# Causal attention heads in a fused trunk: the division by the softmax sums on ScalarE, the second pair's transposes in later steps

## Chip, cores, metric

One Trainium2 chip, one core. The metric is the device time of one execution in microseconds; the kernel before takes 824.06 us (median of 3 runs, 823.75 to 824.91).

## What is computed

Two layers over 256 tokens of width 2048, in float32. Layer 0 mixes by trailing-window pooling, layer 1 by causal attention with 12 heads of 128 (the sequence is one block long, so the block selection of the reference picks nothing, and each query attends to the tokens up to itself). Both layers have a memory branch of 4 heads over 256 memory tokens. Cut to what matters here:

```
s = q @ k.T * HEAD_DIM**-0.5        # layer 1: masked to k_pos <= q_pos
p = softmax(s)
o = p @ v
mixed = concat([branch * silu(gate_b), mem_o * silu(gate_m)])
h = layer_norm(ALPHA * h + mixed @ w_out)
```

The causal heads need q, k, v and a gate from four projections of h; k and v have one shared weight for all B layers.

## The kernel before, in words

**Split products.** A float32 product is made of three matmuls in the type fp32r. Every operand is split by `split` (L69): ScalarE copies it to fp32r (the high part, L71), VectorE subtracts the high part from the original (the low part, L72). A product is then high x high, high x low and low x high. So each weight block passes DMA, ScalarE, VectorE and TensorE.

**Items and steps.** All weights come in items of 128x1024 (512 KB) in one list, in the order in which TensorE uses them. The main loop of `run` (L130) does one step for each item i: it splits item i+3 (LP = 3), issues the load of item i+4 on the SyncE queue (LD = 4, four `raw` buffers), issues item i's matmuls, with the epilogue of a projection if the item is its last, and then calls whatever was registered for this step by `later(n, fn)` (L92), in the order of registration. Each engine takes its instructions in this order. Nothing else orders the work.

**Causal heads.** Layer 1 does the 12 causal heads in three groups of four (the loop that calls `plan` at L686 and L687). A group has eight items for k (`w_sk`), eight for q (`w_in`), eight for the gate (`w_in`), eight for v (`w_sv`, split into the tile `xm`). Step 0 in this text is the last item of q: there `go` registers two pairs of heads, `MobaPair`, through `plan(pr, a, b, c)` (L395). Steps 1 to 8 are then the gate, steps 9 to 16 the values, and from step 17 on come the next group's keys, or after the last group the output projection. A pair has these parts:

- `a` (L353), TensorE, VectorE: scores in PSUM, the mask added (L366), row maxima (L266) and their scaling (L267).
- `exps` (L269), ScalarE: four exponentials with a per-partition bias and a running sum, from p into the tile `ebuf`.
- `divide` (L274), VectorE: one reciprocal of the sums (L275), four multiplications of `ebuf` in place (L277).
- `turn` (L346), VectorE: four transposes of 32x192 for each of four groups of partitions, from `ebuf` to p (L350).
- `b` (L373), ScalarE and VectorE: the split of the transposed probabilities of one head into ph and pl.
- `c` (L380), TensorE: the value products of both heads into o. For each head and each half m of the keys it does value-high x ph, value-high x pl, value-low x ph, so that the third and the sixth matmul are the first to read the low value parts. Then `gated` (L279) multiplies with the gate (L282) and splits into zT.

The first pair has a = 1, b = 6, c = 17, the second a = 7, b = 18, c = 20. The tiles p, ebuf, ph and pl have one buffer each.

**Memory heads.** `MemPair` (L285) has the same parts, but transposes its divided probabilities on TensorE, in `b` (L305). It runs once in each layer (`mem_q_gate`, L515), with `divide` and `gated` shared with the causal heads.

The epilogue of the gate (L232) folds two accumulators (L220 on ScalarE, L221 on VectorE) and in the next step does a tanh (L241) and a product (L242). The epilogue of the values (L247) splits each of two accumulators into the tile vv.

Of the kernel before, what the change touches and what calls it, by code (L numbers as in the profile page):

```python
# [11 lines left out]
F32 = mybir.dt.float32  # L12
F32R = mybir.dt.float32r
AF = mybir.ActivationFunctionType
ALU = mybir.AluOpType
AX = mybir.AxisListType

P = 128
T = 256
# [26 lines left out]
def trunk(ctx: ExitStack, tc: tile.TileContext, a: dict, out: bass.AP):  # L46
    nc = tc.nc
    ctx.enter_context(tc.manual_schedule())
    sb = ctx.enter_context(tc.tile_pool(name="sb", bufs=1))
# [9 lines left out]
    zT = sb.tile([P, KT, 2 * T], F32R, name="zT")  # L59
# [6 lines left out]
    def mm(o, l, r, start, stop):  # L66
        nc.tensor.matmul(o, l, r, start=start, stop=stop)  # L67

    def split(hi, lo, src):  # L69

        nc.scalar.activation(hi, src, AF.Copy)  # L71
        nc.vector.tensor_sub(lo, src, f(hi))  # L72
# [19 lines left out]
    def later(n, fn):  # L92
        events[now[0] + n].append(fn)
# [73 lines left out]
    def proj_t(mov, wblk, done):  # L167


        acc = []  # L170

        def consume(kb):
            def go(wh, wl, k0=0, k1=4):
                if not acc:
                    acc.extend(ps.tile([P, 512], F32, name="acc", bufs=4) for _ in range(2))
                h = wh.rearrange("p (k n) -> p k n", n=256)
                l = wl.rearrange("p (k n) -> p k n", n=256)
                for n in range(2):
                    s = slice(n * P, (n + 1) * P)
                    for kk in range(k0, k1):  # L180
                        k = 4 * kb + kk
                        if k < KT - 1:
                            mm(acc[n], h[:, kk, s], mov[:, k], k == 0, False)
                        mm(acc[n][:, :T], l[:, kk, s], mov[:, k, :T], False, False)
                        if k == KT - 1:
                            mm(acc[n], h[:, kk, s], mov[:, k], False, True)
                    if kb == 3:
                        done(n, acc[n])
            return go
        for kb in range(4):  # L190
            item(wblk[kb], BLK, consume(kb))
# [31 lines left out]
    def to_heads(dst, base):  # L223
        def done(n, acc):
            s = sb.tile([P, T], F32, name="fold", bufs=3)
            hi, lo = dst()[:, base + n, :T], dst()[:, base + n, T:]
            fold(s, acc)
            nc.vector.tensor_copy(hi, s)
            nc.vector.tensor_sub(lo, s, f(hi))
        return done  # L230

    def to_gate(dst, base):  # L232

        def done(n, acc):
            s = sb.tile([P, T], F32, name="fold", bufs=3)
            fold(s, acc)
            g = dst()

            def finish():
                th = sb.tile([P, T], F32, name="th", bufs=2)  # L240
                nc.scalar.activation(th, s, AF.Tanh, scale=0.5)  # L241
                nc.vector.scalar_tensor_tensor(g[:, base + n, :], th, 1.0, s,  # L242
                                               op0=ALU.add, op1=ALU.mult)
            later(1, finish)
        return done

    def to_values(dst):  # L247
        def done(t, acc):
            split(dst()[:, t, 0], dst()[:, t, 1], acc)
        return done  # L250

    def heads_tile(name):
        return sb.tile([P, 4, 2 * T], F32R, name=name)


    class Rows:
# [17 lines left out]
        def divide(self):  # L274
            nc.vector.reciprocal(self.sm, self.sm)  # L275
            for c, (src, dst) in enumerate(self.rows):
                nc.vector.tensor_scalar_mul(dst, dst, self.sm[:, c:c + 1])  # L277

    def gated(o, g, kt):  # L279

        zf = sb.tile([P, T], F32, name="zf", bufs=3)
        nc.vector.scalar_tensor_tensor(zf, o, 0.5, g, op0=ALU.mult, op1=ALU.mult)  # L282
        split(zT[:, kt, :T], zT[:, kt, T:], zf)

    class MemPair(Rows):  # L285
        def __init__(self, h0, st):
# [29 lines left out]
        def c(self):  # L316
            v, g = self.st["v"], self.st["g"]
            o = ps.tile([P, 2, T], F32, name="o")
            for j in range(2):
                h = self.h0 + j  # L320
                for m in range(2):
                    vh = v[:, m, 0, h * HD:(h + 1) * HD]
                    vl = v[:, m, 1, h * HD:(h + 1) * HD]
                    s = slice(m * T, (m + 1) * T)
                    mm(o[:, j], vh, self.ph[:, j, s], m == 0, False)
                    mm(o[:, j], vh, self.pl[:, j, s], False, False)
                    mm(o[:, j], vl, self.ph[:, j, s], False, m == 1)
            for j in range(2):
                gated(o[:, j], g[:, self.h0 + j, :], 12 + self.h0 + j)

    class MobaPair(Rows):

# [47 lines left out]
        def c(self):  # L380
            v, g = self.st["v"], self.st["g"]
            o = ps.tile([P, 2, T], F32, name="o")
            for j in range(2):
                h = self.h0 + j

                for m, (d, s) in enumerate(((o[:, j], slice(0, T)), (o[:, j, P:], slice(T, 384)))):
                    vh = v[:, m, 0, h * HD:(h + 1) * HD]
                    vl = v[:, m, 1, h * HD:(h + 1) * HD]
                    mm(d, vh, self.ph[:, j, s], m == 0, False)
                    mm(d, vh, self.pl[:, j, s], False, False)  # L390
                    mm(d, vl, self.ph[:, j, s], False, m == 1)
            for j in range(2):
                gated(o[:, j], g[:, self.h0 + j, :], self.kt0 + j)

    def plan(pr, a, b, c):  # L395

        later(a, pr.a)
        later(a + 1, pr.exps)
        later(a + 2, pr.divide)
        if isinstance(pr, MobaPair):  # L400
            for i, groups in enumerate(((0,), (1, 2), (3,))):
                later(a + 2 + i, lambda groups=groups: pr.turn(*groups))
        later(b, lambda: pr.b(0))
        later(b + 1, lambda: pr.b(1))
        later(c, pr.c)
# [69 lines left out]
    def fresh(key, make):  # L475

        tiles = []

        def g():
            if not tiles:  # L480
                tiles.append(make())
                st[key] = tiles[0]
            return tiles[0]
        return g
# [16 lines left out]
    def w_in(layer, c):  # L501
        return [a["w_in"][layer, c, kb] for kb in range(4)]

    def after(fn):

        it = items[-1]
        old = it["consume"]

        def go(*w):
            if old is not None:  # L510
                old(*w)
            fn()
        it["consume"] = go

    def mem_q_gate(layer):  # L515
        q = fresh("q", lambda: heads_tile("qq"))
        g = fresh("g", gate_tile)
        for c in range(2):
            proj_t(xT, w_in(layer, 12 + c), to_heads(q, 2 * c))
        prs = [MemPair(0, st), MemPair(2, st)]  # L520

        def go():
            plan(prs[0], 1, 5, 9)
            plan(prs[1], 7, 11, 14)
        after(go)
        for c in range(2):
            proj_t(xT, w_in(layer, 14 + c), to_gate(g, 2 * c))
# [98 lines left out]
    for half in range(2):  # L626
# [3 lines left out]
        g = fresh("g", gate_tile)  # L630
# [43 lines left out]
    for grp in range(3):  # L674
        k = fresh("k", lambda: heads_tile("kk"))
        q = fresh("q", lambda: heads_tile("qq"))
        g = fresh("g", gate_tile)
        v = fresh("v", val_tile)
        for c in range(2):
            proj_t(xT, [a["w_sk"][2 * grp + c, kb] for kb in range(4)], to_heads(k, 2 * c))  # L680
        for c in range(2):
            proj_t(xT, w_in(1, 2 * grp + c), to_heads(q, 2 * c))
        prs = [MobaPair(2 * j, 4 * grp + 2 * j, st) for j in range(2)]

        def go(prs=prs):
            plan(prs[0], 1, 6, 17)  # L686
            plan(prs[1], 7, 18, 20)  # L687
        after(go)
        for c in range(2):
            proj_t(xT, w_in(1, 6 + 2 * grp + c), to_gate(g, 2 * c))  # L690
        proj_n(xT, [a["w_sv"][grp, kb] for kb in range(8)], to_values(v), place=in_mem)
# [58 lines left out]
    def last(t, c0, c1):  # L750
        o = ps.tile([P, 512], F32, name="acc", bufs=4)[:, :c1 - c0]
        for k in range(KT):
            zh = zT[:, k, t * P:(t + 1) * P]
            zl = zT[:, k, T + t * P:T + (t + 1) * P]
            mm(o, zh, kept[0][:, k, c0:c1], k == 0, False)
            mm(o, zh, kept[1][:, k, c0:c1], False, False)
            mm(o, zl, kept[0][:, k, c0:c1], False, k == KT - 1)
        return o
# [26 lines left out]
    o = last(0, 0, 512)  # L785
    nc.vector.bn_aggr(m0, stats[:, 1, :3].rearrange("p a b -> p (a b)"))
    for n in (1, 2):
# [3 lines left out]
    o = last(1, 0, 256)  # L791
# [3 lines left out]
    o = last(1, 256, 512)  # L795
# [14 lines left out]
                                   op0=ALU.mult, op1=ALU.subtract)  # L810
# [70 lines left out]
```

## Time and profile before

| | |
|---|---|
| runs, median (range) | 824.06 us (823.75 to 824.91) |
| the profiled execution | 824.11 us |
| its span, first to last instruction | 822.2 us |
| TensorE matmuls busy | 809.1 us |
| VectorE busy | 593.0 us |
| ScalarE busy | 396.2 us |

The span is what the trace covers; 1.9 us of the execution's time lie around it. "Busy" of an engine is the time in which one of its compute instructions runs. PE is TensorE, DVE VectorE, ACT ScalarE. A row "A <- B" of the waits says that A's engine stood idle until B had ended. A row of a timeline has the start and the length in us; instructions of one kind that follow each other are merged, with their count behind x, and the idle time ahead of them stands in square brackets with what ended it. Two neighbours on an engine can overlap a little, since the next one starts while the last one drains.

### The profile page before, as it was taken

Reading aid. Unit: us, or ns where it says so; the run is one execution under the profiler, and the core shown is the slowest. Engines: PE = TensorE matmul, PEld = TensorE weight load, DVE = VectorE, ACT = ScalarE, POOL = GpSimd, SP = SyncE. Lnnn points to the kernel's source line nnn. Section 1 sums busy time; section 2 is a strip of 40 time slices with the busy share of each in tenths; the row PEclk is TensorE's granted clock in tenths of the full one; section 3 lists DMA queues with packets and bytes.
Section 4 is the critical chain, followed back from the end, with each engine's and each line's share of the span. In section 5 each row is a group of like instructions: output and inputs, shape, how many; then the busy total and the mean of one; then the engine's idle time right before and its main releaser. Section 6 shows DMA issues by size and latency. Waiting matters only on the chain.

```text
span 822.2 us, 11569 instructions
## 1 busy us (share of the span) xinstructions
PE 809.1 (98%) x4410; PEld 697.0 (85%) x4410; DVE 593.0 (72%) x890; ACT 396.2 (48%) x578; POOL 0.2 (0%) x4
## 2 busy tenths in 40 slices
PE   9999999999999999999999999999999999999996
PEld 6888888898888888888888888788878888788885
DVE  5686678667957555797667669875897668968746
ACT  6564555545555343444455445354454445455610
POOL 0000000000000000000000000000000000000000
PEclk9999999999999999999999999999999999999998
DMA  9876446456567655775554554655446654467832
GB/s 328 294 251 204 166 154 201 161 185 215 181 195 279 210 195 189 207 236 198 183 177 147 186 162 150 204 173 193 144 153 205 192 189 133 156 205 234 283 123 102
DMA packets 47163, 159.13 MB, mean 194 GB/s; under 512 B 5375, under 2 KB 7167, under 8 KB 46847
## 3 DMA queue, kind: packets, MB, share of 16 engines
q1 hardware_dynamic: 45792, 155.21, 57.6%
q10 hardware_dynamic: 1316, 3.19, 1.0%
q8 instruction: 34, 0.56, 0.3%
q14 instruction: 21, 0.17, 0.1%
HBM read 156.28 MB, written 2.10 MB: 193 GB/s over the span
## 4 chain that ended last, share of the span: by engine, by line
PE 87%; DVE 10%; ACT 2%; issue 1%; DVEq 0%
PE acc L67 78%; PE o L67 4%; DVE p L350 3%; PE pt L67 2%; DVE xm L72 2%; PE s L67 2%; DVE wl L72 1%; ACT ebuf L271 1%; DVE ebuf L277 1%; DVE gate L242 0%; PE pt L312 0%; DVE nb L266 0%; DVE p L366 0%; ACT wh L71 0%; ACT xm L71 0%
## 5 line engine op out<-in xcount | busy, mean ns | idle before, releaser
L67 PE MATMUL acc<-xm,wh 128*128 128x512 f32 x1344 | 465.8, 394 | 0.0
L72 DVE TENSOR_TENSOR wl<-raw,wh 128x1024 fp32r<-128x1024 f32 (+2 forms) x250 | 295.0, 1187 | 148.9 <-ACT wh L71 147.0
L67 PE MATMUL acc<-xm,wl 128*128 128x256 f32 x1344 | 363.0, 280 | 0.0
L71 ACT ACTIVATE wh<-raw 128x1024 fp32r<-128x1024 f32 (+2 forms) x250 | 255.5, 1028 | 210.1 <-PE acc L67 134.7
L67 PEld LDWEIGHTS acc<-xm,wh 128*128 128x128 f32 x1344 | 247.5, 188 | 49.1 <-ACT wh L71 0.7
L67 PEld LDWEIGHTS acc<-xm,wl 128*128 128x128 f32 x1344 | 253.1, 188 | 7.4 <-DVE wl L72 0.4
L67 PE MATMUL acc<-wh,zT 128*128 128x512 f32 x448 | 139.4, 390 | 0.0
L67 PEld LDWEIGHTS acc<-wh,zT 128*128 128x128 f32 x448 | 84.1, 188 | 17.2
L67 PE MATMUL acc<-wl,zT 128*128 128x512 f32 x224 | 87.3, 390 | 0.0
L67 PE MATMUL acc<-xm 128*128 128x512 f32 x288 | 67.8, 394 | 3.9 <-DVE xm L72 3.9
L67 PEld LDWEIGHTS acc<-xm 128*128 128x128 f32 x288 | 53.4, 188 | 17.7 <-DVE xm L72 6.9
L72 DVE TENSOR_TENSOR xm<-raw,xm 128x1024 fp32r<-128x1024 f32 (+2 forms) x41 | 47.7, 1170 | 10.8 <-ACT xm L71 10.3
L220 ACT ACTIVATE fold<-acc 128x256 f32<-128x256 f32 x72 | 27.6, 384 | 52.6 <-PE acc L67 51.4
L67 PEld LDWEIGHTS acc<-wl,zT 128*128 128x128 f32 x224 | 42.1, 188 | 8.6
L71 ACT ACTIVATE xm<-raw 128x1024 fp32r<-128x1024 f32 (+2 forms) x41 | 41.1, 1010 | 13.8 <-PE acc L67 6.6
L350 DVE STREAM_TRANSPOSE p<-ebuf 32x192 f32<-32x192 f32 x96 | 35.5, 370 | 1.6
L221 DVE TENSOR_TENSOR fold<-acc,fold 128x256 f32<-128x256 f32 x72 | 29.4, 418 | 5.2 <-ACT fold L220 5.2
L71 ACT ACTIVATE zT<-zf 128x256 fp32r<-128x256 f32 x32 | 12.9, 414 | 38.0 <-DVE zf L282 33.7
L67 PE MATMUL acc<-xm,zT 128*128 128x256 f32 (+1 forms) x144 | 22.6, 319 | 0.0
L67 PEld LDWEIGHTS acc<-xm,zT 128*128 128x128 f32 x144 | 20.7, 191 | 1.9
L67 PE MATMUL acc<-wh,xm 128*128 128x512 f32 x64 | 21.6, 404 | 0.0
L72 DVE TENSOR_TENSOR zT<-zf,zT 128x256 fp32r<-128x256 f32 x32 | 12.9, 423 | 9.7 <-ACT zT L71 9.7
(126 smaller groups left out, 505.5 us busy)
## 6 DMA issues: line engine op xcount, KB each, us to landing
raw<-in_w_in SPq DMA_DIRECT2D x128, 512.0 KB, 3.4
raw<-in_w_out SPq DMA_DIRECT2D x64, 512.0 KB, 4.2
raw<-in_w_sk SPq DMA_DIRECT2D x24, 512.0 KB, 4.5
raw<-in_w_sv SPq DMA_DIRECT2D x24, 512.0 KB, 3.3
raw<-in_w_mv SPq DMA_DIRECT2D x14, 512.0 KB, 5.4
raw<-in_w_mk SPq DMA_DIRECT2D x12, 512.0 KB, 4.1
raw<-in_xT SPq DMA_DIRECT2D x4, 512.0 KB, 5.1
res<-in_x ACTq DMA_DIRECT2D x2, 1024.0 KB, 5.4
```

What stands on the lines that cost most here:

```text
L67: nc.tensor.matmul(o, l, r, start=start, stop=stop)
L71: nc.scalar.activation(hi, src, AF.Copy)
L72: nc.vector.tensor_sub(lo, src, f(hi))
L220: nc.scalar.activation(dst, acc[:, T:], AF.Copy)
L221: nc.vector.tensor_add(dst, acc[:, :T], dst)
L271: nc.scalar.activation(dst, src, AF.Exp, bias=self.nb[:, c:c + 1], scale=SCALE, accum_out=self.sm[:, c:c + 1])
L277: nc.vector.tensor_scalar_mul(dst, dst, self.sm[:, c:c + 1])
L350: nc.vector.transpose(p[32 * g:32 * g + 32, h * GX:(h + 1) * GX], e[32 * h:32 * h + 32, g * GX:(g + 1) * GX])
```

## The change

The division moves from VectorE to ScalarE, for causal and memory heads; the reciprocal stays. `plan` takes the steps of the four transpose groups as a list: the first pair's run in steps 4, 5, 5 and 6 in place of 3, 4, 4 and 5, the second pair's in steps 11, 13, 14 and 15 in place of 9, 10, 10 and 11. The first pair's `b` moves from steps 6 and 7 to 7 and 8, the second pair's `a` from 7 to 8, so its exponentials from 8 to 9 and its division from 9 to 10. `gated` takes both heads of a pair at once: both products with the gate first, then both splits.

```diff
         def divide(self):
             nc.vector.reciprocal(self.sm, self.sm)
             for c, (src, dst) in enumerate(self.rows):
-                nc.vector.tensor_scalar_mul(dst, dst, self.sm[:, c:c + 1])
+                nc.scalar.activation(dst, dst, AF.Copy, scale=self.sm[:, c:c + 1])
 
     def gated(o, g, kt):
 
-        zf = sb.tile([P, T], F32, name="zf", bufs=3)
-        nc.vector.scalar_tensor_tensor(zf, o, 0.5, g, op0=ALU.mult, op1=ALU.mult)
-        split(zT[:, kt, :T], zT[:, kt, T:], zf)
+        zfs = [sb.tile([P, T], F32, name="zf", bufs=3) for _ in range(2)]
+        for j, zf in enumerate(zfs):
+            nc.vector.scalar_tensor_tensor(zf, o[:, j], 0.5, g[:, j], op0=ALU.mult, op1=ALU.mult)
+        for j, zf in enumerate(zfs):
+            split(zT[:, kt + j, :T], zT[:, kt + j, T:], zf)
...
-            for j in range(2):
-                gated(o[:, j], g[:, self.h0 + j, :], self.kt0 + j)
-
-    def plan(pr, a, b, c):
+            gated(o, g[:, self.h0:self.h0 + 2], self.kt0)
+
+    def plan(pr, a, turns, b, c):
 
         later(a, pr.a)
         later(a + 1, pr.exps)
         later(a + 2, pr.divide)
-        if isinstance(pr, MobaPair):
-            for i, groups in enumerate(((0,), (1, 2), (3,))):
-                later(a + 2 + i, lambda groups=groups: pr.turn(*groups))
+        for g, t in enumerate(turns):
+            later(t, lambda g=g: pr.turn(g))
         later(b, lambda: pr.b(0))
         later(b + 1, lambda: pr.b(1))
         later(c, pr.c)
...
-            plan(prs[0], 1, 5, 9)
-            plan(prs[1], 7, 11, 14)
+            plan(prs[0], 1, (), 5, 9)
+            plan(prs[1], 7, (), 11, 14)
...
-            plan(prs[0], 1, 6, 17)
-            plan(prs[1], 7, 18, 20)
+            plan(prs[0], 1, (4, 5, 5, 6), 7, 17)
+            plan(prs[1], 8, (11, 13, 14, 15), 18, 20)
```

## Rows read from the trace of the kernel before

**Rows 1.** The page's table of engines: busy us (share of the span) x instructions.

```profile
PE 809.1 (98%) x4410; PEld 697.0 (85%) x4410; DVE 593.0 (72%) x890; ACT 396.2 (48%) x578; POOL 0.2 (0%) x4
```

**Rows 2.** The waits, whole span: us in total, times, longest us.

```profile
PE acc L67 <- DVE xm L72: 3.9, 3, 1.3
```

**Rows 3.** TensorE's timeline, group 0, steps 9 to 18: start us, us.

```profile
505.86 14.30 PE L67 MATMUL acc<-xm 128*128 128x512 f32 x61
521.45 8.32 PE L67 MATMUL acc<-xm 128*128 128x512 f32 x35 [1.28 <-DVE xm L72]
...
532.39 0.28 PE L67 MATMUL o<-ph,vv 128*128 128x256 f32 x1
...
532.91 0.44 PE L67 MATMUL o<-ph,vv 128*128 128x128 f32 x2
...
533.72 0.44 PE L67 MATMUL acc<-xm,wh 128*128 128x512 f32 x1
```

**Rows 4.** VectorE's timeline, group 0, steps 3 to 16: start us, us.

```profile
490.31 1.23 DVE L72 TENSOR_TENSOR wl<-raw,wh 128x1024 fp32r<-128x1024 f32 x1 [1.75 <-ACT wh L71]
491.45 0.17 DVE L275 RECIPROCAL sm<-sm 128x4 f32<-128x4 f32 x1
491.66 1.01 DVE L277 TENSOR_SCALAR ebuf<-ebuf,sm 128x128 f32<-128x128 f32 x4
492.70 1.51 DVE L350 STREAM_TRANSPOSE p<-ebuf 32x192 f32<-32x192 f32 x4
494.24 1.23 DVE L72 TENSOR_TENSOR wl<-raw,wh 128x1024 fp32r<-128x1024 f32 x1
...
496.16 3.05 DVE L350 STREAM_TRANSPOSE p<-ebuf 32x192 f32<-32x192 f32 x8
...
502.06 0.76 DVE L242 SCALAR_TENSOR_TENSOR gate<-th,fold 128x256 f32<-128x256 f32 x2
502.74 1.22 DVE L72 TENSOR_TENSOR xm<-raw,xm 128x1024 fp32r<-128x1024 f32 x1
...
504.34 1.22 DVE L72 TENSOR_TENSOR xm<-raw,xm 128x1024 fp32r<-128x1024 f32 x1
...
506.13 0.96 DVE L366 TENSOR_TENSOR p<-s,mask 128x768 f32<-128x768 f32 x1
...
508.17 0.17 DVE L267 TENSOR_SCALAR nb<-nb 128x4 f32<-128x4 f32 x1
...
511.23 1.23 DVE L72 TENSOR_TENSOR xm<-raw,xm 128x1024 fp32r<-128x1024 f32 x1 [1.08 <-ACT xm L71]
...
520.17 1.23 DVE L72 TENSOR_TENSOR xm<-raw,xm 128x1024 fp32r<-128x1024 f32 x1
521.42 1.53 DVE L350 STREAM_TRANSPOSE p<-ebuf 32x192 f32<-32x192 f32 x4
...
529.81 1.32 DVE L72 TENSOR_TENSOR vv<-acc,vv 128x512 fp32r<-128x512 f32 x2
```

**Rows 5.** ScalarE's timeline, group 0, steps 2 to 9: start us, us.

```profile
488.25 0.49 ACT L271 ACTIVATE ebuf<-p,nb 128x256 f32<-128x256 f32 x1
...
492.16 0.39 ACT L220 ACTIVATE fold<-acc 128x256 f32<-128x256 f32 x1 [0.40 <-PE acc L67]
...
508.38 0.40 ACT L271 ACTIVATE ebuf<-p,nb 128x128 f32<-128x128 f32 x1 [1.93 <-DVE nb L267]
...
510.15 1.04 ACT L71 ACTIVATE xm<-raw 128x1024 fp32r<-128x1024 f32 x1
511.10 0.71 ACT L241 ACTIVATE th<-fold 128x256 f32<-128x256 f32 x2
```

**Rows 6.** The page's DMA issues: KB each, median us from issue to landing.

```profile
raw<-in_w_sk SPq DMA_DIRECT2D x24, 512.0 KB, 4.5
```

**Rows 7.** VectorE's timeline, layer 1's second memory pair: start us, us.

```profile
439.64 0.17 DVE L275 RECIPROCAL sm<-sm 128x4 f32<-128x4 f32 x1
```

**Rows 8.** The chain that ended last, the same pair: start us, us.

```profile
442.57 0.44 PE pt L312 x4
```

More of the change, by code (lines that the diff above doesn't have):

```diff
@@ L327, in c @@
                     mm(o[:, j], vl, self.ph[:, j, s], False, m == 1)
-            for j in range(2):
-                gated(o[:, j], g[:, self.h0 + j, :], 12 + self.h0 + j)
+            gated(o, g[:, self.h0:self.h0 + 2], 12 + self.h0)
     class MobaPair(Rows):
@@ L391, in c @@
                     mm(d, vl, self.ph[:, j, s], False, m == 1)
-            for j in range(2):
-                gated(o[:, j], g[:, self.h0 + j, :], self.kt0 + j)
-    def plan(pr, a, b, c):
+            gated(o, g[:, self.h0:self.h0 + 2], self.kt0)
+    def plan(pr, a, turns, b, c):
         later(a, pr.a)
```

## The prediction

> **What bounds the kernel now.** I read the page's table of engines first: TensorE is busy for 98% of the span [rows 1], so a change pays only where TensorE waits. The list of waits names one wait inside the work that this change touches: matmuls into acc stand still for a VectorE subtraction on xm, 3.9 us in 3 times [rows 2], one for each group of four causal heads. The other groups repeat group 0 at +96.0 and +191.9 us, so everything is worked out in group 0.
>
> I count steps n of the main loop from the last item of the query projection; "high n" and "low n" are ScalarE's copy and VectorE's subtraction issued in step n, which serve TensorE's item n+3. TensorE's timeline [rows 3] shows items 9 to 13 and the first matmul of item 14 without a gap: 61 matmuls from 505.86, 14.30 us, so (14.30-0.39)/60 = 0.232 each and 2.78 an item. The 62nd, the first that needs a low half, was due at 520.01 and starts at 521.45: 1.44 us lost (the row's 1.28 leaves out the drain of the pipeline). Low 11 runs from 520.17 for 1.23 us and ends the wait. VectorE's timeline [rows 4] shows why it is late: after step 3 it has hardly a hole, only 1.08 us before low 9.
>
> The end of this stage matters too. TensorE starts the first pair's value product at 532.39, its sixth matmul (the first on the second half of the value tile's low part) at 532.91, and the next item at 533.72. VectorE makes both low parts of the value tile in one run of 1.32 us from 529.81, so by 531.13: 1.8 us to spare, no more.
>
> **The change, part by part.** (a) Division. VectorE loses four multiplications per pair, 491.66 to 492.70, 1.04 us. ScalarE gains four copies of 2x128 and 2x256 columns with a per-partition scale. No row shows such a copy. Upper bound: the exponentials on the same tiles together with the reads of their sums, 510.15-508.38 = 1.77 us [rows 5]. Lower bound: a copy without a per-partition operand, 0.39 us at 256 columns, and 0.28 at 128 (estimate by the slope from it to 1.04 at 1024 columns); with the overlap of 0.09 seen between neighbours (510.15+1.04 against 511.10) that is 2x0.30+2x0.19 = 0.98. I take the exponentials alone, 0.49 and 0.40, since they too have a per-partition operand: 2x0.40+2x0.31, about 1.40. The Trainium skill differs within itself here. Its page "VectorE: DVE Perf Modes", in the section on the TRN2 errata, gives ScalarE 224 cycles and one per column, from which, with the same overlap, I estimate 1.0 us and a total near 825. Its page "ScalarE: Activation LUTs", section "What ACT_TABLE_LOAD costs", adds some 93 ns for each per-partition operand, from which I estimate 1.39 and the total forecast here. The exponentials' rows lie at the second, but no row of before shows such a copy itself.
>
> The larger price is the hand-over. High n+1 stands behind the divisions in ScalarE's queue, the divisions behind VectorE's reciprocal, and VectorE has nothing between the reciprocal and low n+1. So for each pair it stands still for 1.40+1.04 and two hand-overs of about 0.04 (491.45+0.17 to 491.66): 2.5 us, to save 1.04.
>
> (b) The schedule, step by step on both queues; pitches are differences of neighbouring starts in [rows 4]: subtraction to next 1.14 (to a transpose 1.25), four transposes 1.54, two folds 0.78, two gates 0.68.
> - Step 3: reciprocal 491.45, divisions 491.66 to 493.06, high 4 to 494.10, low 4 at 494.15 (494.24 before).
> - Steps 4 to 6: folds 495.29, one transpose group 496.07, low 5 497.62, two groups 498.87, gates 501.97, low 6 502.65, last group 503.90, low 7 505.45.
> - Steps 7 and 8: first pl 506.58, low 8 507.05, folds 508.20, second pl 508.98, mask 509.63 (from subtraction to mask 1.79-1.14), scaled maxima 2.04 later: 511.67, where 508.17 stands now.
> - Step 9: low 9 511.75 (no hole before it now). ScalarE: exponentials 511.87, two tanh 513.64, high 10 at 514.25 (tanh 0.71-0.09).
> - Step 10: low 10 515.34, reciprocal 516.48, divisions 516.69, high 11 518.09 to 519.13.
> - Step 11: low 11 519.18 to 520.41, against 520.17 to 521.40 before.
> TensorE's wait at item 14 shrinks from 1.44 to about 0.45, a gain of 1.0 us. Low 12 then ends at 523.21, just when item 15 asks (523.23).
>
> (c) The second pair's 16 transposes now stand behind low 11, where 12 of them stood ahead. From 519.18 VectorE works through without a hole: low 11, group (520.43), low 12, low 13, group (524.37), low 14, group (527.17), low 15, group (529.97), low 16 (531.52), value parts from 532.66 to 533.98. What hides loads there: low 9 to 12 release the load buffers of items 16 to 19, used four high halves later, against 4.5 us from issue to landing [rows 6].
> TensorE, 1.0 us earlier, reaches the value product at 531.39. Its third matmul needs the first low value part (533.35), its sixth the second: 534.02 instead of 531.91, 2.1 us lost. The next item starts 0.81 later, at 534.83 against 533.72 now.
>
> Sum per group: -1.0 + 2.1 = +1.1 us. Behind that point VectorE has three items (8.3 us) to catch up; the second pair's pl, after its four subtractions and both products, still precede the product of step 20.
>
> (d) Memory pairs: divisions 4x0.40 = 1.6 us in place of 1.1 on VectorE. Even from today's reciprocal at 439.64 [rows 7] they end at 441.5, before the transposes on TensorE at 442.57 [rows 8]; high and low halves slip by under 2 us, covered by their lead of three items. Without that cover 1.6 us per pair. Cost 0.
> (e) The order in gated(), and the scores one step later: the splits behind the products are first read items later, the second pair's scores are the same matmuls behind item 8 instead of 7. Cost 0; the cover is the same lead.
>
> Three groups: 3 x 1.1 = 3.3 us. The profiled execution took 824.11 (its span 822.2 and 1.9 around it), 0.05 over the median of 824.06; either gives **827.4 us**.
> Bounds: each 0.1 us in a division's price moves low 11, and with it the value parts and the next item, by 0.2 per group. At 0.98 low 11 starts 0.84 earlier, net +0.27 a group, 824.9. At 1.77 it starts 0.74 later, net +1.85, 829.6.
>
> **Rivals.**
> 1. Faster: VectorE is not late at the value parts. Place: low 11. At 518.07 instead of 519.18 the two waits cancel; at 516.63 neither is left, and the time is 824.06 - 3x1.44 = 819.7. Mechanism: ScalarE's divisions would have to run in the shadow of other VectorE work, as they do before transposes when the step between holds ready work. For it: the transposes themselves wait for nothing now, and 2.1 us of VectorE work go. Against: both engines take their queues in order in every row, and low 11 follows high 11, high 11 the divisions.
> 2. No change: the divisions cost the lower bound, 0.98, and the wait merely moves from item 14 to the value product: 824.9. For it: a plain copy's row. Against: the exponentials'.
> 3. The first wait isn't removed: the second pair's maxima come 3.5 us later than now, and if the divisions take 1.77 or more, low 11 is back at 520 and both waits stand, 829.6 to 830.5. For it: the margin at item 14 is already negative. Against: no row has an ACTIVATE of this size above 0.5 us.
>
> **How the numbers follow.** A measurement of this kernel can tell about 0.2% (1.65 us) from no change: 822.4 to 825.7. Forecast 0.60, rival 1 0.13, rival 2 0.17, rival 3 0.10. Slower: forecast and rival 3, 0.70; same 0.17; faster 0.13. The range leaves out rival 1 and the far end of rival 3: 823.6 to 829.6, from just under rival 2 to the upper bound of the divisions.
>
> **What would show it.** Right: the subtraction for item 14 starts near 519.2 in group 0, the wait of acc for xm falls from 3.9 to about 1 us, and a new wait of o for vv's subtraction appears, 3 times, near 2 us each with the drain; VectorE idles 2 to 2.5 us behind both reciprocals; ScalarE's divisions start 0.3 to 0.4 us apart. Wrong: no wait at o, or low 11 before 518, would mean that the holes do not open; a wait of TensorE in the memory pairs would mean (d) was mis-costed.

## The result and the profile after

The changed kernel takes 829.66 us (median of 4 runs, 828.26 to 830.14), the kernel before 824.26 in the same comparison: a ratio of 1.0062, 95% interval 1.0045 to 1.008. It is slower by 5.4 us. The forecast was slower, 827.4; the range, 823.6 to 829.6, ends 0.06 us below the median (the ratio, applied to the 824.06 us that the forecast starts from, gives 829.2). The profiled execution took 828.26 us, with a span of 826.5.

The table of engines after answers to [rows 1]: VectorE has 11 us less to do, ScalarE 13 more.

```profile
PE 810.8 (98%) x4410; PEld 698.5 (85%) x4410; DVE 582.0 (70%) x850; ACT 408.8 (49%) x618; POOL 0.2 (0%) x4
```

TensorE's waits after, over the span (us in total, times, longest), answer to [rows 2]. The wait of acc for xm has shrunk from 3.9 to 1.4 us. A new one has come: the value product o waits for VectorE's part of the value tile, once in each group, longer than the old wait was.

```profile
PE o L67 <- DVE vv L72: 4.7, 3, 1.6
...
PE acc L67 <- DVE xm L72: 1.4, 3, 0.5
```

TensorE's timeline in group 0 (start us, us, idle before) answers to [rows 3]:

```profile
505.92 14.00 PE L67 MATMUL acc<-xm 128*128 128x512 f32 x61
520.37 8.31 PE L67 MATMUL acc<-xm 128*128 128x512 f32 x35 [0.46 <-DVE xm L72]
528.52 0.39 PE L67 MATMUL acc<-xm,wh 128*128 128x512 f32 x1
...
531.29 0.28 PE L67 MATMUL o<-ph,vv 128*128 128x256 f32 x1
531.41 0.28 PE L67 MATMUL o<-pl,vv 128*128 128x256 f32 x1
533.22 0.44 PE L67 MATMUL o<-ph,vv 128*128 128x256 f32 x2 [1.53 <-DVE vv L72]
533.50 0.27 PE L67 MATMUL o<-pl,vv 128*128 128x128 f32 x1
533.82 0.49 PE L67 MATMUL o<-ph,vv 128*128 128x128 f32 x2
...
534.67 0.45 PE L67 MATMUL acc<-xm,wh 128*128 128x512 f32 x1
```

Item 14's second matmul, the first to need low 11, starts at 520.37 instead of 521.45. TensorE reaches the value product 1.10 us earlier (531.29 against 532.39), stands there for the third and the sixth matmul, and starts the next item at 534.67 instead of 533.72.

VectorE's timeline in the same stretch answers to [rows 4]:

```profile
491.53 0.17 DVE L275 RECIPROCAL sm<-sm 128x4 f32<-128x4 f32 x1
494.27 1.23 DVE L72 TENSOR_TENSOR wl<-raw,wh 128x1024 fp32r<-128x1024 f32 x1 [2.57 <-ACT wh L71]
...
516.35 0.17 DVE L275 RECIPROCAL sm<-sm 128x4 f32<-128x4 f32 x1
519.10 1.23 DVE L72 TENSOR_TENSOR xm<-raw,xm 128x1024 fp32r<-128x1024 f32 x1 [2.57 <-ACT xm L71]
520.24 1.50 DVE L351 STREAM_TRANSPOSE p<-ebuf 32x192 f32<-32x192 f32 x4
...
532.48 1.28 DVE L72 TENSOR_TENSOR vv<-acc,vv 128x512 fp32r<-128x512 f32 x2
```

Behind each reciprocal VectorE stands still for 2.57 us. The row names the high half (ScalarE's copy) as what ended the hole. The high half was not slow itself: ScalarE's timeline shows what it stood behind. The divisions wait 1.44 us for the reciprocal, take 1.40 (516.62 to the next start at 518.02), and only then come the high halves.

```profile
491.79 1.49 ACT L277 ACTIVATE ebuf<-ebuf,sm 128x128 f32<-128x128 f32 x4 [1.44 <-DVE sm L275]
...
516.62 1.49 ACT L277 ACTIVATE ebuf<-ebuf,sm 128x128 f32<-128x128 f32 x4 [1.44 <-DVE sm L275]
518.02 2.94 ACT L71 ACTIVATE xm<-raw 128x1024 fp32r<-128x1024 f32 x3
```

In group 1 the same wait costs more than in group 0. The chain that ended last (start us, us) shows the three items behind it, 48 matmuls, once in 8.40 and once in 9.96 us:

```profile
534.83 8.40 PE acc L67 x48
...
631.72 9.96 PE acc L67 x48
```

The windows of group 1 tell why. Columns: length, busy us (x instructions) of PE, of TensorE's weight loads (PEld), of DVE, ACT and POOL, then the granted clock in parts of 2.4 GHz, the DMA share, GB/s. TensorE is busy for 0.53 us in the window of the wait. One window later the granted clock has fallen: two windows stand at 0.53 and 0.62, a mix of the half level, 1.2 GHz, with the full one, and the third is back at 1.00.

```profile
628.00:630.00 2.00, 0.53 (x4) 0.30 (x2) 1.97 (x4) 0.00 (x0) 0.00 (x0) 1.00 0.58 231
630.00:632.00 2.00, 1.87 (x13) 1.68 (x14) 2.00 (x4) 0.00 (x0) 0.00 (x0) 1.00 0.76 252
632.00:634.00 2.00, 2.00 (x8) 1.72 (x8) 1.34 (x5) 1.79 (x4) 0.00 (x0) 0.53 0.63 219
634.00:636.00 2.00, 2.00 (x9) 1.67 (x9) 1.63 (x2) 0.32 (x1) 0.00 (x0) 0.62 0.16 59
636.00:638.00 2.00, 2.00 (x13) 1.75 (x13) 0.82 (x1) 1.47 (x2) 0.00 (x0) 1.00 0.75 262
```

So there are two questions for the experiments: whether the division's place, the moved transposes or both make VectorE late, and whether the fall of the clock belongs to the new wait. Theory: the hand-over from the reciprocal over ScalarE to the next low half makes VectorE late, and TensorE pays for that at the value product, with the clock on top. Rival: the transposes that now stand behind step 11 make the value parts late, whoever divides. A second rival: the fall of the clock has nothing to do with the wait.

### The profile page after: what moved, and what is told of

Its sections match the earlier page's. It is cut to its first block, busy times and chain, and to the rows that moved or that the text cites. A ratio compares the mean times of both kernels' runs of the same rounds, so it can differ in the third digit from the quotient of the medians.

```text
span 826.5 us, 11570 instructions
## 1 busy us (share of the span) xinstructions
PE 810.8 (98%) x4410; PEld 698.5 (85%) x4410; DVE 582.0 (70%) x850; ACT 408.8 (49%) x618; POOL 0.2 (0%) x4
## 4 chain that ended last, share of the span: by engine, by line
PE 80%; DVE 10%; ACT 4%; issue 4%; DMA 1%; SPq 0%; DVEq 0%; ACTq 0%
PE acc L67 72%; DVE p L351 4%; PE o L67 4%; PE pt L67 2%; PE s L67 2%; DVE xm L72 2%; DVE wl L72 1%; ACT ebuf L271 1%; ACT ebuf L277 1%; ACT wh L71 1%; DVE nb L266 1%; DVE p L367 1%; ACT xm L71 1%; DMA raw<-in_w_mk 1%; DVE fold L221 1%
## 5 line engine op out<-in xcount | busy, mean ns | idle before, releaser
L67 PE MATMUL o<-ph,vv 128*128 128x256 f32 (+1 forms) x80 | 16.1, 281 | 4.8 <-DVE vv L72 4.7
```

## The experiments

### 1. The division back on VectorE, all else as changed

```diff
-                nc.scalar.activation(dst, dst, AF.Copy, scale=self.sm[:, c:c + 1])
+                nc.vector.tensor_scalar_mul(dst, dst, self.sm[:, c:c + 1])
```

> The changed kernel with one thing undone: the four multiplications by the reciprocal are on VectorE again; the new steps of the transposes, of the second pair and the new order in gated() stay. Theory (the hand-over reciprocal -> ScalarE -> next low half holds VectorE up): without the two holes of 2.57 us the subtraction of step 11 starts near 516.2 in group 0 instead of 519.10, both low value parts are done near 530.9, before TensorE asks, and neither wait is left: 824.06 - 3 x 1.44 = 819.7 us, granted clock 1.00 throughout. Rival (the transposes moved behind step 11 are what makes VectorE late, whoever divides): the wait of o for vv stays near 1.5 us, three times, and the time stays at 827 or above.

Measured: 818.15 us (817.89 to 818.59), ratio to before 0.9925 (0.9913 to 0.9938). Both waits of the groups are gone from the list of waits. TensorE's timeline has all 96 matmuls of the values in one piece and goes through the value product; VectorE's has the subtraction of step 11 at 515.86 and the value parts at 529.24.

```profile
505.92 21.93 PE L67 MATMUL acc<-xm 128*128 128x512 f32 x96
527.69 0.39 PE L67 MATMUL acc<-xm,wh 128*128 128x512 f32 x1
...
530.46 0.28 PE L67 MATMUL o<-ph,vv 128*128 128x256 f32 x1
...
530.70 0.34 PE L67 MATMUL o<-ph,vv 128*128 128x256 f32 x2
...
531.79 0.44 PE L67 MATMUL acc<-xm,wh 128*128 128x512 f32 x1
```
```profile
514.93 1.01 DVE L277 TENSOR_SCALAR ebuf<-ebuf,sm 128x128 f32<-128x128 f32 x4
515.86 1.22 DVE L72 TENSOR_TENSOR xm<-raw,xm 128x1024 fp32r<-128x1024 f32 x1
...
529.24 1.28 DVE L72 TENSOR_TENSOR vv<-acc,vv 128x512 fp32r<-128x512 f32 x2
```

The rival falls: with the same 16 transposes behind step 11 the value parts are in time. The expected time was 1.5 us too high, which shows a number of the prediction to be too small. One matmul takes (21.93-0.39)/95 = 0.227 us here, not the 0.232 read from [rows 3]. From the first matmul of item 9 to the next item behind the product the kernel before takes 533.72-505.86 = 27.86 us, this one 531.79-505.92 = 25.87. So the kernel before loses 1.99 us per group, not 1.44.

Of the 0.55 us more, 0.30 lie inside the 61 matmuls: 14.30 us, against 60 x 0.227 + 0.39 = 14.01. This is a wait shorter than a matmul's drain, so that the matmuls' rows do not list it as idle. The rows of TensorE's weight loads (PEld) in the kernel before do: they stand idle for VectorE's subtraction at item 13, and then at item 14.

```profile
517.11 2.63 PEld L67 LDWEIGHTS acc<-xm 128*128 128x128 f32 x12 [0.38 <-DVE xm L72]
521.45 2.63 PEld L67 LDWEIGHTS acc<-xm 128*128 128x128 f32 x12 [1.71 <-DVE xm L72]
```

The 0.38 are an upper figure, since the record of a load can be missing. In experiment 1 the weight loads have no wait for xm at all. Another 0.2 lie in the 35 matmuls behind the wait, 8.32 us against 34 x 0.227 + 0.39 = 8.11. The changed kernel has them too (8.31), behind a wait a third as long; what they are made of is not shown.

### 2. The division alone on ScalarE, in the old steps

```diff
-                nc.vector.tensor_scalar_mul(dst, dst, self.sm[:, c:c + 1])
+                nc.scalar.activation(dst, dst, AF.Copy, scale=self.sm[:, c:c + 1])
```

> The kernel before with the division alone moved to ScalarE; all steps and gated() as before. Theory: the transposes stand right behind the division, so VectorE has a hole of about 1.6 us where it spent 1.04 on the multiplications, 0.6 later per pair; the subtraction of step 11 starts 1.2 later than before and the wait at item 14 grows from 1.44 to about 2.6 us: 824.06 + 3 x 1.2 = 827.7 us, more if the granted clock falls after the longer wait. Rival (moved transposes to blame): 1 us of VectorE work per pair is saved and the time is 824 or less.

Measured: 828.35 us (828.19 to 828.82), ratio 1.0051 (1.0035 to 1.0066). The waits:

```profile
PE acc L67 <- DVE xm L72: 7.1, 6, 1.3
...
PE pt L312 <- DVE pl L72: 0.9, 2, 0.4
```

The hole ahead of the transposes is 1.62 us, as expected. The wait for xm grows from 3.9 to 7.1, not as one longer wait but at two items of each group. The groups repeat every 97.1 us in place of 96.0, 3.3 us in all. The second row was not expected: in each layer the second memory pair's transposes wait on TensorE for a late pl, 0.43 us of idle and about 0.6 with the drain (the two sets of transposes start 3.83 us apart, 3.23 in the kernel before). VectorE's timeline there has a hole of 2.15 us behind the reciprocal.

```profile
440.24 0.17 DVE L275 RECIPROCAL sm<-sm 128x4 f32<-128x4 f32 x1
442.56 0.76 DVE L242 SCALAR_TENSOR_TENSOR gate<-th,fold 128x256 f32<-128x256 f32 x2 [2.15 <-ACT th L241]
```

3.3 and 2 x 0.6 make 4.5, with 4.3 measured. The rival falls: the work saved on VectorE is no gain.

### 3. The new order in gated() alone

```diff
-        zf = sb.tile([P, T], F32, name="zf", bufs=3)
-        nc.vector.scalar_tensor_tensor(zf, o, 0.5, g, op0=ALU.mult, op1=ALU.mult)
-        split(zT[:, kt, :T], zT[:, kt, T:], zf)
+        zfs = [sb.tile([P, T], F32, name="zf", bufs=3) for _ in range(2)]
+        for j, zf in enumerate(zfs):
+            nc.vector.scalar_tensor_tensor(zf, o[:, j], 0.5, g[:, j], op0=ALU.mult, op1=ALU.mult)
+        for j, zf in enumerate(zfs):
+            split(zT[:, kt + j, :T], zT[:, kt + j, T:], zf)
...
```

> The kernel before with the new order in gated() alone (both gate products, then both splits). Theory and rivals alike: nothing that TensorE waits for hangs on it, 824.06 within 0.3 us. If it moves by more, the part (e) of the prediction was mis-costed.

Measured: 824.09 us (10 runs), ratio 1.0000 (0.9991 to 1.001), and TensorE's waits are those of before. Alone it does nothing. The changed kernel has no wait of pt for pl, experiment 2 with the old order has one in each layer: with the division on ScalarE the new order very likely is what keeps the memory pairs free. The traces point that way: the second pair's reciprocal in layer 1 starts at 438.75 here and at 438.81 in the changed kernel, against 439.64 before, so the new order brings it forward by some 0.8 us. But that pair of parts was not run by itself.

### 4. The value product of the first pair one step later

```diff
-            plan(prs[0], 1, (4, 5, 5, 6), 7, 17)
+            plan(prs[0], 1, (4, 5, 5, 6), 7, 18)
```

> The changed kernel with one number changed: the first pair's value product goes from step 17 to step 18, 2.78 us later on TensorE, so that the low value parts, ready near 533.8 in group 0, are there first. Division on ScalarE and all holes stay. Theory (the wait at the value product is the loss, and the fall of the granted clock follows from it): only the wait of about 0.46 at item 14 is left, 824.06 - 3 x 0.98 = 821.1 us, granted clock 1.00 in the steps behind 17. Rival (the fall of the granted clock has nothing to do with this wait): the wait goes and the clock still falls somewhere behind step 17, 822.7 to 824.5 us.

Measured: 820.33 us (820.15 to 820.76), ratio 0.9953 (0.994 to 0.9965), granted clock 0.997 over the span against 0.994 in the changed kernel's profile. In the groups only the wait at item 14 is left:

```profile
PE acc L67 <- DVE xm L72: 1.4, 3, 0.5
```

ScalarE still divides and both holes are there; what cost the time was that TensorE met the late value parts. With the wait the fall of the clock is gone too. By the corrected count a group loses 0.83 us ahead of the product: the changed kernel takes 528.52-505.92 = 22.60 us for the 96 matmuls of the values, experiment 1 takes 527.69-505.92 = 21.77. 818.15 + 3 x 0.83 = 820.6, near the measured 820.33.

### 5. The division on ScalarE, issued behind the next high half

```diff
             nc.vector.reciprocal(self.sm, self.sm)
+
+        def scale(self):
             for c, (src, dst) in enumerate(self.rows):
...
         later(a + 2, pr.divide)
+        later(a + 3, pr.scale)
```

> The changed kernel with ScalarE's four divisions issued one step after the reciprocal, behind the next high half in ScalarE's queue. ScalarE still divides; only what stands behind the division differs. Theory (the hole is the hand-over, not the price of a division): VectorE's hole of 2.57 us behind each reciprocal goes, at most some 0.7 us stays ahead of the first transposes, TensorE waits nowhere in the groups, 818.2 us as with the division on VectorE. Rival (ScalarE is too slow a place for these divisions, wherever they stand): VectorE's transposes wait for them instead, the value parts stay late, 824 us or more.

Measured: 818.33 us (817.77 to 818.6), ratio 0.9926 (0.9913 to 0.9938), no wait in the groups. VectorE's timeline:

```profile
515.65 0.17 DVE L275 RECIPROCAL sm<-sm 128x4 f32<-128x4 f32 x1
515.74 1.19 DVE L72 TENSOR_TENSOR xm<-raw,xm 128x1024 fp32r<-128x1024 f32 x1
517.44 1.51 DVE L353 STREAM_TRANSPOSE p<-ebuf 32x192 f32<-32x192 f32 x4 [0.51 <-ACT ebuf L279]
```

The same four divisions on the same engine, with the same 1.40 us, cost nothing that these times can tell: low 11 starts 0.09 us after the reciprocal's start, the divisions run beside it, and 0.51 us of the hole is left ahead of the transposes. Ahead of the first pair's it is 0.95 us, more than the 0.7 expected, and it does no harm either. So it is the place in ScalarE's queue that costs, not the engine.

### 6. The value product one step earlier

```diff
-            plan(prs[0], 1, (4, 5, 5, 6), 7, 17)
+            plan(prs[0], 1, (4, 5, 5, 6), 7, 16)
```

> The changed kernel with the first pair's value product one step earlier, step 16, so that TensorE waits for the low value parts some 4.8 us in each group instead of 1.8. Theory (the granted clock falls to its lower level behind such a wait, now and then behind 1.8 us, surely behind a longer one): without the clock 818.15 + 3 x (0.83 + 4.82) = 835.1 us; with a fall in each group, at 1.57 us each as in the changed kernel's profile, 839.8 us, granted clock near 0.5 for about 3.5 us behind each of the three waits. Rival (the fall has nothing to do with the wait): 835.1 us, or one fall at another place, 836.7.

Measured: 841.31 us (840.71 to 842.25), ratio 1.0205 (1.0189 to 1.022). The wait is 4.32 us in group 0, 3.50 (behind another of 0.54 for ScalarE's value part) and 4.31 in the others, and the clock falls in all three groups; two windows of group 0, the one with no matmul and one behind it:

```profile
530.00:532.00 2.00, 0.00 (x0) 0.00 (x0) 1.93 (x5) 0.00 (x0) 0.00 (x0) 0.91 0.74 262
...
534.00:536.00 2.00, 2.00 (x10) 1.90 (x10) 0.31 (x1) 0.00 (x0) 0.00 (x0) 0.50 0.58 229
```

Without the clock the expectation was 835.1; the other (841.31-835.1)/3 = 2.1 us per group are more than the 1.57 taken from the changed kernel. Here the product itself runs at the lower level, too: from its third matmul to the next item group 0 takes 535.45-533.26 = 2.19 us, against 534.67-533.22 = 1.45 in the changed kernel. The rival, a fall that has nothing to do with the wait, does not hold: in the kernel before and in experiments 1 to 5 and 7, none of which waits at the product, the granted clock is 1.00 in every window of the groups; here it falls behind each wait.

### 7. The second pair's transposes in the new steps, nothing else

```diff
-            plan(prs[0], 1, 6, 17)
-            plan(prs[1], 7, 18, 20)
+            plan(prs[0], 1, (3, 4, 4, 5), 6, 17)
+            plan(prs[1], 7, (11, 13, 14, 15), 18, 20)
...
```

The cut part makes `plan` take the list of steps, as in the change.

> The kernel before with one part of the change: the second pair's transposes in steps 11, 13, 14 and 15. Division on VectorE, the first pair, the second pair's scores and gated() as before. Theory: the subtraction of step 11 starts 3 x 1.54 earlier than in the kernel before, near 515.6 in group 0, no wait is left at item 14, and the low value parts are done near 530.2, before they are asked for: 818.2 us, all of the gain. Rival (the transposes moved behind step 11 make the value parts late by themselves): a wait of o for vv, 820 us or more.

Measured: 818.28 us (818.0 to 818.32), ratio 0.9925 (0.9913 to 0.9937), no wait in the groups. Low 10 and low 11 run as one piece, so that low 11 starts at 514.24 + 2.36 - 1.23 = 515.37, and the transposes follow:

```profile
514.24 2.36 DVE L72 TENSOR_TENSOR xm<-raw,xm 128x1024 fp32r<-128x1024 f32 x2
516.51 1.51 DVE L350 STREAM_TRANSPOSE p<-ebuf 32x192 f32<-32x192 f32 x4
...
528.76 1.28 DVE L72 TENSOR_TENSOR vv<-acc,vv 128x512 fp32r<-128x512 f32 x2
```

This part alone brings some 6 us, all that the groups' waits held; its time cannot be told apart from those of experiments 1 and 5.

### 8. The changed kernel, a second profile

No edit.

> The changed kernel unchanged, for a second profile. Theory: without any fall of the clock 818.15 + 3 x 2.88 = 826.8 us, plus 1.57 us for each group in which the granted clock falls behind the wait at the value product: 828.3 us with one such group, 829.9 with two, 831.5 with three, and the windows show as many. Rival: the time differs by falls elsewhere, or without any.

Measured: 829.6 us, one run, with falls in groups 1 and 2:

```profile
632.00:634.00 2.00, 2.00 (x7) 1.64 (x7) 1.33 (x4) 1.72 (x4) 0.00 (x0) 0.50 0.73 195
...
732.00:734.00 2.00, 2.00 (x6) 1.52 (x6) 1.58 (x2) 0.80 (x2) 0.00 (x0) 0.50 0.51 193
```

The chain's 48 and 36 matmuls behind the three waits:

```profile
534.91 8.39 PE acc L67 x48
...
631.78 9.96 PE acc L67 x48
...
730.20 9.83 PE acc L67 x36
```

In the first profile the last of these took 8.24, so a fall costs 1.56 to 1.59 us. 818.15 + 3 x (0.83 + 2.05) = 826.8, where 2.05 is what the product takes (534.67-531.29 = 3.38) beyond the 1.33 that it takes in the kernel before (533.72-532.39). One fall makes 828.4, two 829.9. The profiled 828.26 and 829.6 are these two cases. The other runs of the changed kernel, 829.64 to 830.14, agree with two falls, but they have no profile that would show them.

## Why the prediction was right, and what it missed

The direction and the mechanism held, step by step:
- (a) The divisions' price: 1.40 us taken, 1.40 measured; the hole 2.5 taken, 2.57 measured (0.09 to ScalarE, 1.40, the high half's 1.04, 0.04 back). Rival 2 rested on 0.98 and falls. Of the two estimates from the Trainium skill, the one from the page "ScalarE: Activation LUTs", section "What ACT_TABLE_LOAD costs", with its extra for each per-partition operand (1.39), agrees with the trace; the one from "VectorE: DVE Perf Modes", section on the TRN2 errata (1.0), does not.
- (b) Low 11 was put at 519.18 and starts at 519.10. The gain up to the value product was put at 1.0 us and is 1.10.
- (c) The value parts were put at 532.66 and start at 532.48; the wait was put at 2.1 us and is 2.05; the next item was put at 534.83 and starts at 534.67. Net 1.1 a group was forecast; 0.95 came in group 0, of which 0.06 lies ahead of the group (505.92 against 505.86): 0.9.
- (d) and (e) cost nothing in the changed kernel, as forecast; experiment 3 shows (e) by itself. But (d) leaned on a cover that was not named: experiment 2 finds 0.6 us per layer when the division goes to ScalarE without the new order in gated().

What was missed is a term of the sum. The forecast let TensorE go on at full speed behind its new wait. In one group or two of the three the granted clock falls to 1.2 GHz behind it, some 1.57 us each: 3 x 0.9 = 2.7 and one or two falls make 4.3 or 5.8, where 3.3 was forecast and 5.4 measured. That is why the median lies at the far end of the range.

By its number alone the median would fit rival 3, 829.6 to 830.5, too. Its mechanism did not come: it needed divisions of 1.77 us or more, low 11 back at 520 and both waits in full. Measured were 1.40, 519.10, and 1.4 of the 3.9 us left of the first wait.

A second size was off, without an effect on the sign: the wait before, step one of the prediction, is not 1.44 but 1.99 us per group, since the 61 matmuls read as gapless contain a short wait (0.30) and the 35 behind the long one lose another 0.2. So rival 1's full gain is not 819.7 but 818.15. Rival 1 named its deciding point rightly, low 11 by 516.63: in experiments 1, 5 and 7 it starts at 515.86, 515.74 and 515.37, and no wait is left. Its mechanism, divisions in the shadow of ready work, is what experiment 5 does and the change does not.

Of the change's parts, then: the new steps of the second pair's transposes gain some 6 us alone. The division's place costs 11.5 us on top of the new steps (829.66 against 818.15): 3 x 0.83 at item 14, 3 x 2.05 at the value product and one or two falls of the clock. In the old steps it costs 4.3 (experiment 2), so its price depends on what stands behind it on VectorE. The order in gated() does nothing by itself. What each of the two holes costs was not run apart.

## What to carry to other kernels

Moving work from a full engine to one with room costs the hand-over, not only the instruction: look at what stands behind the moved instruction in the new engine's queue, and whether the old engine waits for just that. Where the answer is needed late, issue it behind the work that the other engine needs next. And follow a late engine to every point where TensorE meets it: here the first wait was shortened, and the next point, which had 1.8 us to spare, became the dearer one.

## What the runs showed of the hardware that was not expected

- TensorE's granted clock fell to 1.2 GHz behind waits of 1.53 to 1.58 us at the value product in three of six groups seen, and behind waits of 3.5 to 4.3 us in three of three; behind waits of 1.3 us (the kernel before) or 0.5 us (experiment 4) in none. The length does not tell which of the six it was: the clock fell behind 1.56, 1.56 and 1.57, and not behind 1.53, 1.54 and 1.58. What decides it is not shown. Each fall behind the shorter wait cost 1.56 to 1.59 us, as much as the idle time itself.
- A run of matmuls that the timeline merges can contain waits shorter than the drain of a matmul: 61 of them took 14.30 us before and 14.00 after, 0.232 and 0.227 each. The rows of the weight loads list that wait (517.11, at most 0.38 us), the rows of the matmuls do not.
